# A decoder trunk in float32: the tokens' 1/rms moved from h^T to the projections' results, and the first projection begun K tile by K tile

## The chip, the cores and the metric

One core of one Trainium2 chip runs the whole kernel in one launch. The metric is the device time in microseconds, the median of several runs.

## The reference

Four residual layers on x (256 tokens by 1024 columns, float32). Layers 0 and 3 are of kind A (gated), layer 1 is attention (B), layer 2 pooling (C). What matters here is the norm and kind A:

```python
def rms_norm(x, g):
    y = x * lax.rsqrt(jnp.mean(x * x, axis=-1, keepdims=True) + EPS)
    return y * g

def mixer_a(h, w_in, v_gain, w_s, b_s, w_out):          # h = rms_norm(x, norm_gain[i])
    proj = h @ w_in                                     # 1024 -> 3 * 2048
    u, v, z = ...                                       # 2048 columns each
    v = rms_norm(v, v_gain)
    mixed = jnp.einsum('gij,bcjgd->bcigd', ws, v) + b_s # 8 groups, 128 x 128 lower triangular
    y = u * mixed * jax.nn.silu(z)
    return y @ w_out                                    # x = x + this
```

A token's 1/rms is one number per row of h. It commutes with h @ w_in: a row of the result may be multiplied by it instead.

## The kernel before

**Products.** Every float32 product is made of three matmuls on rounded parts (`mm3`, L75): high by high (L77), high by low (L78), low by high (L79). `hi_of` (L81, ScalarE) makes a high part, `lo_of` (L84, VectorE) the low part from the source and the high one. The stationary operand is a 128x128 tile of h^T (a K tile `k` of 8 and a token block `t` of 2), the moving one 512 columns of weights.

**Weights.** The host lays all weights out as a stream of 272 units of 128x1024 (512 KB): two K tiles of 512 columns each. `load_units` (L127) starts a unit's transfer on SP's queue into one of four raw buffers (`wr`), `split_hi` (L137) makes its high part, `split_units` (L147) its low part and starts the transfer of the unit four further on. `wNh` and `wNl` are the parts of unit N. A projection of 512 columns uses four units, and `step` (L163) keeps the splitting a few units ahead.

**Order.** The program text sets the order of every engine's queue; nothing is reordered on the chip between engines' instructions of one queue. Small generators (`spawn`, `tick`) put the work behind a projection between the products of the next ones.

**The norm.** For each token block: squares of both halves of x on ScalarE (`half_ss`, L205), the sum (L210), the power -1/2 on GpSimd (L212), the scaling of both halves on VectorE (`norm_scale`, L218, tile `xs`), eight transposes on TensorE into PSUM (L227, tile `hp`), then per K tile the high part with the norm's gain on ScalarE (L232) and the low part on VectorE (L235), both into `hT`.

**The start.** SP's queue holds x of token block 0 in two halves, units 0 and 1, x of block 1 in two halves, units 2 and 3. TensorE runs 24 warm-up transposes of the identity (`WARM`). The norm of block 0 is written out with the splitting of units 0 to 4 between its parts (`between`), block 1's norm follows behind `split_hi(3)` and on. The first projection, columns 0 to 511 of v, is skewed (`proj_tok` with `skew`, L259): all eight K tiles of block 0 first, then all eight of block 1; block 1's transposes (`first_t1`) are put in after three ticks, behind the products with unit 2. The loads of v's gain, W_s and b_s (`load_a`, L343) are on GpSimd's queue.

**Layer A.** `v_task` (L367) squares v on ScalarE (L372) and multiplies it by the gain into `vv` (L373), of which high and low parts are made; after the fourth block of columns, GpSimd's power (L392) gives v's 1/rms, which scales W_s into high and low parts `wsr` (L397, L399). `mix_task` multiplies these with v. z goes through Silu (L456). `y_task` multiplies u by silu(z) (L430) and by the mixed v (L433), turns and splits the result for the output projection (`proj_out`, L297).

Of the kernel before, what the change touches and what calls it, by code (L numbers as in the profile page):

```python
# [17 lines left out]
P = 128  # L18
# [23 lines left out]
MIX_LAG = 4  # L42
LAST_LAG = 1
LAST_AHEAD = 3
WARM = 24


@with_exitstack
def hybrid_trunk_kernel(ctx, tc, x, wts, norm_gainT, a_v_gain, a_wsT, a_bsT, b_gl, b_gv, c_scaleT,
# [121 lines left out]

    xt = [cp.tile([P, D], F32, tag=f"x{t}", name=f"x{t}") for t in range(2)]

    def load_x(t):
        for n in range(2):
            nc.sync.dma_start(xt[t][:, n * HALF:(n + 1) * HALF], x[t * P:(t + 1) * P, n * HALF:(n + 1) * HALF])

    load_x(0)
    load_units(2)
    load_x(1)  # L180
    load_units(RAW_BUFS)
    ident = cp.tile([P, P], F32, tag="ident", name="ident")
    make_identity(nc, ident)
    m05_row = cp.tile([P, 32], F32, tag="m05", name="m05")
    nc.gpsimd.memset(m05_row, -0.5)
    m05 = m05_row[:, :4]
    junk = cp.tile([P, HALF + 32], BF16, tag="junk", name="junk")[:, :HALF]
    hT = cp.tile([P, 2 * KT * S + 16], F32R, tag="hT", name="hT")

    def h_parts(layer):  # L190

        o = 16 if layer in (0, DEPTH - 1) else 0
# [22 lines left out]
    def norm_scale(layer, t, r, engs=(nc.vector, nc.vector)):  # L215
        xs = cp.tile([P, 2, HALF], F32, tag="xs", name=f"xs{layer}{t}", bufs=1)
        for n in range(2):
            engs[n].tensor_scalar(xs[:, n], xt[t][:, n * HALF:(n + 1) * HALF], r[:, 0:1], None, op0=ALU.mult)  # L218
        return xs

    def norm_transpose(layer, t, xs):

        pts = []
        for n in range(2):
            pt = (trp if n else atp)(f"hp{layer}{t}{n}").rearrange("p (k c) -> p k c", c=P)
            for k in range(4):
                nc.tensor.transpose(pt[:, k], xs[:, n, k * P:(k + 1) * P], ident)  # L227
            pts.append(pt)
        sl = slice(t * P, (t + 1) * P)
        hTh, hTl = h_parts(layer)  # L230
        for k in range(KT):
            nc.scalar.activation(hTh[:, k, sl], pts[k // 4][:, k % 4], AF.Copy, scale=gT[:, layer, k:k + 1])  # L232
            yield k
        for k in range(KT):
            nc.vector.scalar_tensor_tensor(hTl[:, k, sl], pts[k // 4][:, k % 4], gT[:, layer, k:k + 1],  # L235
                                           hTh[:, k, sl].bitcast(F32), op0=ALU.mult, op1=ALU.subtract)
            yield KT + k

    def norm_task(layer, t, ss):
# [43 lines left out]
    def proj_feat(name):
# [57 lines left out]


    def load_a(layer, j):  # L343
        kc = cp.tile([P, 3 * D], F32, tag="kc", name=f"kc{layer}")
        wsT = kc[:, 2 * D:].rearrange("p (g c) -> p g c", c=P)
        nc.gpsimd.dma_start(kc[:, :2 * D], a_v_gain[j:j + 1, :].partition_broadcast(P))
        nc.gpsimd.dma_start(wsT, a_wsT[j])
        bsT = cp.tile([P, 24], F32, tag="bs", name=f"bs{layer}")[:, :8]
        nc.gpsimd.dma_start(bsT, a_bsT[:, j])

        for g in range(8):
            nc.gpsimd.affine_select(out=wsT[:, g], in_=wsT[:, g], pattern=[[1, P]], compare_op=ALU.is_ge,  # L352
                                    fill=0.0, base=0, channel_multiplier=-1)
        return kc, wsT, bsT

    def layer_a(layer, consts, pl, mid):
        hcur[:] = h_parts(layer)
        kc, wsT, bsT = consts

        def tmp(tag, name, bufs):  # L360
            return pl.tile([P, HALF], F32, tag=tag, name=name, bufs=bufs)
# [5 lines left out]
        def v_task(n, o):  # L367
# [54 lines left out]
        def y_task(n, up, us):  # L422
# [24 lines left out]
            done.add(("y", layer, n))  # L447

        for n in range(4):
            spawn(v_task(n, proj_tok(f"v{layer}{n}", skew=layer if n == 0 else None)))  # L450
# [412 lines left out]
        proj_out(layer, 16, get)  # L863


    sss = [tiny(2, f"ss_{t}") for t in range(2)]
    for n in range(2):
        half_ss(0, n, sss[0])
    r = norm_rms(0, 0, sss[0])
    split_hi(1)  # L870
    xs = norm_scale(0, 0, r)
    split_units(1)
    r1 = []

    def between(i):
        if i == 3:
            split_hi(2)
        if i == 7:
            split_hi(3)
            for n in range(2):  # L880
                half_ss(1, n, sss[1])
            split_hi(4)
        if i == KT + 1:
            split_units(2)
        if i == KT + 5:
            split_units(3)
            r1.append(norm_rms(0, 1, sss[1]))
        if i == KT + 7:
            r1.append(norm_scale(0, 1, r1[0]))
            split_units(4)  # L890

    for i in norm_transpose(0, 0, xs):
        between(i)
    done.add(("h", 0, 0))
    xs = r1[1]

    def first_t1():
        for i in norm_transpose(0, 1, xs):
            pass
        done.add(("h", 0, 1))  # L900
        yield 1

    spawn(first_t1(), 3)
    consts = load_a(0, 0)
    box = {}

    def after_ws():
        spawn(load_b())

    with tc.tile_pool(name="L0", bufs=1, reuse_waits="tile") as pl:  # L910
        layer_a(0, consts, pl, after_ws)
    with tc.tile_pool(name="L1", bufs=1, reuse_waits="tile") as pl:
        layer_b(1, box["b"], pl)
    with tc.tile_pool(name="L2", bufs=1, reuse_waits="tile") as pl:
        consts = load_a(3, 1)
        layer_c(2, pl)
    with tc.tile_pool(name="L3", bufs=1, reuse_waits="tile") as pl:
        layer_a(3, consts, pl, lambda: None)


    last = {}
# [134 lines left out]
```

## Time and profile before

| what | us |
|---|---|
| median of 3 runs | 845.04 (844.78 to 845.10) |
| profiled execution, its own time | 844.66 |
| its span, first to last instruction | 842.9 |
| TensorE busy | 831.3 |
| VectorE busy | 546.5 |
| ScalarE busy | 488.6 |
| GpSimd busy | 57.6 |

The span is what the profile shows; 1.8 us of the execution's time lie outside it. Times in rows are microseconds from the span's start, and "mean ns" is of one instruction. An instruction's duration runs from its start to its result, so that neighbours on one engine overlap; the distance from one start to the next is what it costs in a full queue. The mean granted clock over the span was 0.999 of full speed.

### The profile page before, as it was taken

To read this page: it belongs to the slowest core of one execution; us is meant where nothing else is said; L and a number is where in the kernel's file an instruction comes from. 1 tells how busy PE (TensorE), PEld (TensorE's weight loads), DVE (VectorE), ACT (ScalarE), POOL (GpSimd) and SP (SyncE) were. 2 spreads that over 40 slices of the span, in tenths; PEclk is the share of its full clock that TensorE was granted. 3 is DMA by queue.
4 is the path that set the end of the run, shared out by engine and by line. 5 is a ranking of instruction groups with operands and counts; after the bars stand their busy time and mean duration, and the time that the engine had idled before them with its cause. 6 is when DMAs were issued, how large, how long until landed. Compare 5 with 4: busy or idle time off the path is not lost.

```text
span 842.9 us, 12424 instructions
## 1 busy us (share of the span) xinstructions
PE 831.3 (99%) x4600; PEld 718.2 (85%) x4600; DVE 546.5 (65%) x932; ACT 488.6 (58%) x918; POOL 57.6 (7%) x79
## 2 busy tenths in 40 slices
PE   8999999999999999999999999999999999999998
PEld 6888888888988888888888889999988888888886
DVE  6876556646747667667668576798754776556551
ACT  7665444336758677677678567446543666434340
POOL 1301000001001021021021012000000000000000
PEclk9999999999999999999999999999999999999999
DMA  8766564552754346345345267546664466454541
GB/s 303 271 203 224 190 198 164 187 193 84 254 174 163 112 147 179 121 151 175 126 150 173 78 220 252 181 150 229 218 204 149 138 245 208 158 183 167 175 149 51
DMA packets 41500, 149.57 MB, mean 177 GB/s; under 512 B 4864, under 2 KB 4880, under 8 KB 41184
## 3 DMA queue, kind: packets, MB, share of 16 engines
q1 hardware_dynamic: 40320, 144.72, 51.8%
q0 software_dynamic: 976, 4.05, 1.4%
q8 instruction: 36, 0.59, 0.3%
q14 instruction: 24, 0.20, 0.1%
q10 hardware_dynamic: 144, 0.02, 0.0%
HBM read 147.72 MB, written 1.05 MB: 176 GB/s over the span
## 4 chain that ended last, share of the span: by engine, by line
PE 86%; ACT 7%; DVE 2%; issue 2%; POOL 2%; DMA 0%; POOLq 0%; DVEq 0%; ACTq 0%
PE wo L77 6%; PE wo L79 6%; PE wo L78 6%; PE qk L79 4%; PE qk L77 4%; PE qk L78 4%; PE z L79 3%; PE z L77 3%; PE u L77 3%; PE z L78 3%; PE u L78 3%; PE u L79 3%; PE v L78 3%; PE v L79 3%; PE v L77 3%; ACT junk L508 2%
## 5 line engine op out<-in xcount | busy, mean ns | idle before, releaser
L513 POOL TENSOR_TENSOR qr<-qm,m 128x4 f32<-128x4 f32 x24 | 30.3, 1272 | 224.2 <-DVE qm L512 224.2
L517 ACT ACTIVATE qn<-qk,qr 128x128 f32<-128x128 f32 x96 | 27.5, 382 | 15.1 <-POOL qr L513 15.1
L508 ACT ACTIVATE junk<-qk 128x128 bf16<-128x128 f32 x96 | 26.8, 279 | 7.3 <-PE qk L79 4.6
L430 DVE TENSOR_TENSOR sz<-u,sz 128x512 f32<-128x512 f32 x16 | 11.0, 685 | 28.2 <-PE u L79 28.2
L232 ACT ACTIVATE hT<-hp,gT 128x128 fp32r<-128x128 f32 x64 | 17.5, 383 | 16.1 <-PE hp L227 16.1
L212 POOL TENSOR_TENSOR r<-ms,m 128x1 f32<-128x1 f32 x8 | 5.4, 670 | 284.8 <-DVE ms L210 284.8
L327 DVE TENSOR_TENSOR x<-wo,x 128x512 f32<-128x512 f32 x16 | 11.0, 690 | 20.1 <-PE wo L79 20.0
L235 DVE SCALAR_TENSOR_TENSOR hT<-hp,gT,hT 128x128 fp32r<-128x128 f32 x64 | 17.9, 343 | 7.7 <-ACT hT L232 7.7
L372 ACT ACTIVATE junk<-v 128x512 bf16<-128x512 f32 x16 | 9.6, 600 | 17.8 <-PE v L79 17.6
L508 ACT ACTIVATION_READ_ACCUMULATOR junk<-qk 128x1 f32 x96 | 19.1, 199 | 0.0
L373 DVE TENSOR_TENSOR vv<-v,kc 128x512 f32<-128x512 f32 x16 | 10.8, 688 | 12.4 <-ACT junk L372 12.2
L526 DVE TENSOR_TENSOR ra<-qn,kcb 128x64 f32<-128x64 f32 x48 | 10.6, 221 | 12.0 <-ACT qn L517 10.9
L456 ACT ACTIVATE sz<-z 128x512 f32<-128x512 f32 x16 | 9.5, 598 | 15.3 <-PE z L79 14.7
L538 PE MATMUL qt<-ident,qn 128*128 128x128 f32 x96 | 14.6, 274 | 3.4 <-DVE qk12l L546 0.5
L538 PEld LDWEIGHTS qt<-ident,qn 128*128 128x128 f32 x96 | 11.3, 140 | 7.3 <-issue 2.7
L205 ACT ACTIVATE junk<-x 128x512 bf16<-128x512 f32 x16 | 10.2, 639 | 11.0 <-DVE x L327 9.4
L433 DVE SCALAR_TENSOR_TENSOR yy<-mx,bs,sz 128x256 f32<-128x256 f32 x32 | 14.0, 480 | 0.6
L608 ACT ACTIVATE p<-p,rl 128x384 f32<-128x384 f32 (+1 forms) x16 | 11.5, 769 | 4.8 <-DVE rl L607 4.8
L530 DVE TENSOR_TENSOR rb<-qn,kcb 128x32 f32<-128x32 f32 x96 | 13.7, 183 | 0.0
L604 ACT ACTIVATE p<-p,nb 128x768 f32<-128x768 f32 x8 | 7.5, 938 | 7.9 <-DVE nb L603 7.9
L512 DVE TENSOR_SCALAR qm<-qs 128x4 f32<-128x4 f32 x24 | 3.3, 164 | 12.8 <-ACT junk L508 12.8
L352 POOL TENSOR_SCALAR_AFFINE_SELECT kc<-kc 128x128 f32<-128x128 f32 x16 | 10.0, 659 | 14.1 <-DMA kc<-in_a_wsT_dram 14.1
(2770 smaller groups left out, 3257.8 us busy)
## 6 DMA issues: line engine op xcount, KB each, us to landing
wr<-in_wts_dram SPq DMA_DIRECT2D x272, 512.0 KB, 4.1
kc<-in_a_v_gain_dram POOLq DMA_DIRECT2D x2, 1024.0 KB, 6.4
x<-in_x_dram SPq DMA_DIRECT2D x4, 256.0 KB, 4.7
kc<-in_a_wsT_dram POOLq DMA_DIRECT2D x2, 512.0 KB, 8.2
out_dram<-x SPq DMA_DIRECT2D x4, 256.0 KB, 2.0
kcb<-in_masks_dram POOLq DMA_DIRECT2D x1, 576.0 KB, 8.0
kcb<-in_b_gl_dram POOLq DMA_DIRECT2D x1, 192.0 KB, 5.9
kcb<-in_rope_dram POOLq DMA_DIRECT2D x1, 64.0 KB, 7.9
```

The source lines that it names most:

```text
L77: nc.tensor.matmul(out_ap, lh[0], rh[0], start=start, stop=False, skip_group_check=True)
L78: nc.tensor.matmul(out_ap, lh[0], rh[1], start=False, stop=False, skip_group_check=True)
L79: nc.tensor.matmul(out_ap, lh[1], rh[0], start=False, stop=stop, skip_group_check=True)
L232: nc.scalar.activation(hTh[:, k, sl], pts[k // 4][:, k % 4], AF.Copy, scale=gT[:, layer, k:k + 1])
L235: nc.vector.scalar_tensor_tensor(hTl[:, k, sl], pts[k // 4][:, k % 4], gT[:, layer, k:k + 1], hTh[:, k, sl].bitcast(F32), op0=ALU.mult, op ...
L433: nc.vector.scalar_tensor_tensor(y[:, sl], mxs[n][t][:, sl], bsT[:, 2 * n + gg:2 * n + gg + 1], us[t][:, sl], op0=ALU.add, op1=ALU.mult)
L508: nc.scalar.activation(junk[:, :HD], ov[t][:, h], AF.Square, accum_out=ssq[t][:, h:h + 1])
L513: nc.gpsimd.tensor_tensor(rq[t], ms, m05, op=ALU.pow)
L517: nc.scalar.activation(qn[t][:, h], ov[t][:, h], AF.Copy, scale=rq[t][:, h:h + 1])
L530: nc.vector.tensor_tensor(rb[:, hs, s0:s0 + 16], qn[t][:, hs, s1:s1 + 16], c, op=ALU.mult)
L538: nc.tensor.transpose(pts[t][:, h], qn[t][:, h], ident)
L608: nc.scalar.activation(f, f, AF.Copy, scale=rl[i][:, 0:1])
```

## The change

In the gated layers (0 and 3) h^T is made of x itself with the norm's gain, without the tokens' 1/rms: `norm_scale` returns x. The 1/rms, kept in two columns beside the constant -0.5 (`r_rows`), goes to the results: as the scale of the squares of v, into the factor of W_s (a product of two 1/rms on GpSimd), as the scale of Silu, and into the product of u and silu(z).

In layer 0 the norm then no longer stands ahead of the first products. `proj_first` writes the first projection out: x's first halves of both token blocks are turned, then K tile by K tile the high and low parts of h^T and of the weights (halves of units 0 and 1) are made and both token blocks' products issued; then the second halves are turned, and units 2 and 3 follow whole. The squares and powers come behind. SP's queue takes x's first halves and the halves of unit 0 in turn, then unit 1, then x's second halves; the first 512 columns of v's gain move to SP's queue behind unit 3, and the other constants of layer 0 are loaded after `proj_first`. The warm-up has 13 transposes instead of 24.

```diff
-WARM = 24
+WARM = 13
...
-    load_x(0)
+    raws.append(wp.tile([P, 2, HALF], F32, tag="wr", name="wr0", bufs=RAW_BUFS))
+    loaded[0] += 1
+    for t in range(2):
+        load_x(t, 0)
+        nc.sync.dma_start(raws[0][:, t], wts[0].rearrange("p (k n) -> p k n", n=HALF)[:, t])
     load_units(2)
-    load_x(1)
+    for t in range(2):
+        load_x(t, 1)
     load_units(RAW_BUFS)
+    kc_first = cp.tile([P, 3 * D], F32, tag="kc", name="kc0")
+    nc.sync.dma_start(kc_first[:, :HALF], a_v_gain[0:1, :HALF].partition_broadcast(P))
...
-        r = tiny(1, f"r{layer}{t}")
+        r = r_rows[t] if gated(layer) else tiny(1, f"r{layer}{t}")
+        r_tok[t] = r
...
+    def norm_scale(layer, t, r):
+        if gated(layer):
+            return xt[t].rearrange("p (n c) -> p n c", c=HALF)
...
+    def proj_first(name):
...
+        for t in range(2):
+            turn(t, 0)
+        for u in range(2):
+            w_pair(u)
+            for kk in range(2):
+                k = 2 * u + kk
+                if u == 0:
+                    high(0, 0) if k == 0 else high(1, 1)
+                    high(0, 1) if k == 0 else None
+                    w_high(0, kk)
+                    high(1, 0) if k == 0 else None
+                else:
+                    high(0, k)
+                    high(1, k)
+                    w_high(1, kk)
+                w_low(u, kk)
+                for t in range(2):
+                    low(t, k)
+                products(k)
+        for t in range(2):
+            turn(t, 1)
+        for u in range(2, 4):
+            for k in (2 * u, 2 * u + 1):
+                high(0, k)
+                high(1, k)
+            split_hi(u + 1)
+            split_units(u + 1)
+            for k in (2 * u, 2 * u + 1):
+                low(0, k)
+                low(1, k)
+                products(k)
+        used[0] += 4
+        split_units(5)
+        for t in range(2):
+            ss = tiny(2, f"ss_{t}")
+            for n in range(2):
+                half_ss(t, n, ss)
+            norm_rms(0, t, ss)
+        split_units(6)
+        for t in range(2):
+            done.add(("h", 0, t))
+        for _ in range(8):
+            tick()
+        return o
...
-                nc.scalar.activation(junk, o[t], AF.Square, accum_out=vs[t][:, n:n + 1])
+                nc.scalar.activation(junk, o[t], AF.Square, scale=r_tok[t][:, 0:1], accum_out=vs[t][:, n:n + 1])
...
-                rs.append(r)
+                rr = tiny(1, f"vrr{layer}{t}")
+                nc.gpsimd.tensor_tensor(rr, r, r_tok[t], op=ALU.mult)
+                rs.append(rr)
...
-                nc.vector.tensor_tensor(us[t], up[t], us[t], op=ALU.mult)
+                nc.vector.scalar_tensor_tensor(us[t], up[t], r_tok[t][:, 0:1], us[t], op0=ALU.mult, op1=ALU.mult)
...
-                nc.scalar.activation(sz, zp[t], AF.Silu)
+                nc.scalar.activation(sz, zp[t], AF.Silu, scale=r_tok[t][:, 0:1])
```

`turn` issues the four transposes of a half, `high` and `low` a K tile's parts of h^T, `w_high` and `w_low` those of half a unit, `products` the two blocks' six matmuls of a K tile.

**TensorE, the start of the program, before.** `warm` is the warm-up, `hp000` and `hp001` the turned first and second half of block 0's scaled x, `v00_0` the first projection's PSUM bank of token block 0.

```order
L199 MATMUL warm_87<-ident_78 128x128 x24
L227 MATMUL hp000_131<-ident_78,xs00_125 128x128 x4
L227 MATMUL hp001_136<-ident_78,xs00_125 128x128 x4
L77 MATMUL v00_0_202<-w0h_122,hT_86 128x512
L78 MATMUL v00_0_202<-w0l_123,hT_86 128x512
L79 MATMUL v00_0_202<-w0h_122,hT_86 128x512
```

The same place now; `hp000` and `hp010` are the first halves of blocks 0 and 1, and the transposes read x.

```order
L213 MATMUL warm_90<-ident_81 128x128 x13
L241 MATMUL hp000_111<-ident_81,x0_64 128x128 x4
L241 MATMUL hp010_116<-ident_81,x1_65 128x128 x4
L77 MATMUL v00_0_109<-w0h_121,hT_89 128x512
L78 MATMUL v00_0_109<-w0l_122,hT_89 128x512
L79 MATMUL v00_0_109<-w0h_121,hT_89 128x512
L77 MATMUL v00_1_110<-w0h_121,hT_89 128x512
```

The transposes of the second halves have left this place (they now stand behind the products with unit 1), and block 1's products alternate with block 0's.

**ScalarE, from unit 1 to unit 5, before.** L205 are the squares of x.

```order
L82 ACTIVATE w1h_145<-wr1_70 128x1024
L232 ACTIVATE hT_86<-hp001_136,gT_112 128x128 x4
L82 ACTIVATE w2h_152<-wr2_74 128x1024
L205 ACTIVATE junk_85,ss_1_115<-x1_65 128x512 x2
L82 ACTIVATE w3h_157<-wr3_76 128x1024
L232 ACTIVATE hT_86<-hp010_222,gT_112 128x128 x4
L232 ACTIVATE hT_86<-hp011_227,gT_112 128x128 x4
L82 ACTIVATE w4h_260<-wr4_129 128x1024
L82 ACTIVATE w5h_272<-wr5_163 128x1024
```

The same place now; `hp001` and `hp011` are the second halves. The two rows of h^T parts come twice ahead of w2h and twice ahead of w3h (once each shown ahead of w2h).

```order
L82 ACTIVATE w1h_149<-wr1_71 128x512
L245 ACTIVATE hT_89<-hp001_177,gT_104 128x128
L245 ACTIVATE hT_89<-hp011_182,gT_104 128x128
...
L82 ACTIVATE w2h_191<-wr2_75 128x1024
...
L82 ACTIVATE w3h_217<-wr3_77 128x1024
L82 ACTIVATE w4h_239<-wr4_139 128x1024
L219 ACTIVATE junk_88,ss_0_245<-x0_64 128x512 x2
L219 ACTIVATE junk_88,ss_1_251<-x1_65 128x512 x2
L82 ACTIVATE w5h_257<-wr5_167 128x1024
```

w2h and w3h now stand behind the parts of h^T that the transposes release, and the squares of both blocks behind w4h.

**VectorE, from unit 4 to unit 7, before.** `vv` is v times its gain, `v00l` its low part.

```order
L85 TENSOR_TENSOR w4l_261<-wr4_129,w4h_260 128x1024
L85 TENSOR_TENSOR w5l_273<-wr5_163,w5h_272 128x1024
L85 TENSOR_TENSOR w6l_285<-wr6_170,w6h_284 128x1024
L373 TENSOR_TENSOR vv000_298<-v00_0_202,kc0_184 128x512
L373 TENSOR_TENSOR vv001_299<-v00_1_203,kc0_184 128x512
L85 TENSOR_TENSOR v00l_297<-vv000_298,v00h_296 128x512
L85 TENSOR_TENSOR v00l_297<-vv001_299,v00h_296 128x512
L85 TENSOR_TENSOR w7l_315<-wr7_182,w7h_314 128x1024
```

The same place now:

```order
L85 TENSOR_TENSOR w4l_240<-wr4_139,w4h_239 128x1024
L224 SCALAR_TENSOR_TENSOR ms00_248<-ss_0_245 128x1
L224 SCALAR_TENSOR_TENSOR ms01_254<-ss_1_251 128x1
L85 TENSOR_TENSOR w5l_258<-wr5_167,w5h_257 128x1024
L476 TENSOR_TENSOR vv000_279<-v00_0_109,kc0_79 128x512
L476 TENSOR_TENSOR vv001_280<-v00_1_110,kc0_79 128x512
L85 TENSOR_TENSOR v00l_278<-vv000_279,v00h_277 128x512
L85 TENSOR_TENSOR v00l_278<-vv001_280,v00h_277 128x512
L85 TENSOR_TENSOR w6l_296<-wr6_195,w6h_295 128x1024
```

The sums of the squares have moved in front of w5l, and w6l has moved behind the evacuation of the first projection (on ScalarE w6h likewise).

## Rows read from the trace of the kernel before

**Rows 1.** Page, part 1: busy us (share of span) x instructions.
```profile
PE 831.3 (99%) x4600; PEld 718.2 (85%) x4600; DVE 546.5 (65%) x932; ACT 488.6 (58%) x918; POOL 57.6 (7%) x79
```

**Rows 2.** View of waits, TensorE: us in total, times, longest.
```profile
PE qt L538 <- DVE qk12l L546: 0.5, 1, 0.5
...
PE v L78 <- DVE w2l L85: 0.5, 1, 0.5
```

**Rows 3.** Chain of waits, first 26 us: start, us, what.
```profile
0.81 3.17 DMA x<-in_x_dram
...
4.00 0.73 ACT junk L205 x2
...
14.95 1.14 DVE w3l L85
```

**Rows 4.** Timeline, TensorE, first 25 us: start, us, instruction [idle before].
```profile
1.43 4.39 PE L199 MATMUL warm<-ident 128*128 128x128 f32 x24 [1.43 <-POOL ident masks.py:199]
6.95 1.09 PE L227 MATMUL hp<-ident,xs 128*128 128x128 f32 x8 [1.13 <-DVE xs L218]
8.07 0.51 PE L77 MATMUL v<-w0h,hT 128*128 128x512 f32 x1
...
16.47 0.40 PE L79 MATMUL v<-w3h,hT 128*128 128x512 f32 x1
...
22.84 0.39 PE L77 MATMUL v<-w4h,hT 128*128 128x512 f32 x1
```

**Rows 5.** Windows of TensorE: stretch, busy (count), PEclk, DMA share, GB/s.
```profile
2.40:3.40 1.00, 1.00 (x6) 1.00 0.97 312
4.70:5.70 1.00, 1.00 (x10) 1.00 1.16 299
...
838.90:840.90 2.00, 0.00 (x0) 1.00 0.23 88
840.90:842.90 2.00, 0.00 (x0) 0.51 0.11 43
```

**Rows 6.** Timeline, ScalarE, first 25 us.
```profile
7.65 1.14 ACT L232 ACTIVATE hT<-hp,gT 128x128 fp32r<-128x128 f32 x4
8.66 1.07 ACT L82 ACTIVATE w1h<-wr 128x1024 fp32r<-128x1024 f32 x1
9.61 1.16 ACT L232 ACTIVATE hT<-hp,gT 128x128 fp32r<-128x128 f32 x4
...
23.68 0.62 ACT L82 ACTIVATE v00h<-vv 128x512 fp32r<-128x512 f32 x1
```

**Rows 7.** VectorE: groups by form (busy, mean ns | idle), then timeline.
```profile
L235 DVE SCALAR_TENSOR_TENSOR hT<-hp,gT,hT 128x128 fp32r<-128x128 f32 x16 | 4.5, 343 | 0.4 <-ACT hT L232 0.4
L85 DVE TENSOR_TENSOR v00l<-vv,v00h 128x512 fp32r<-128x512 f32 x2 | 1.4, 696 | 0.1
...
11.95 1.22 DVE L85 TENSOR_TENSOR w2l<-wr,w2h 128x1024 fp32r<-128x1024 f32 x1
...
26.15 1.23 DVE L85 TENSOR_TENSOR w7l<-wr,w7h 128x1024 fp32r<-128x1024 f32 x1 [0.26 <-ACT w7h L82]
```

**Rows 8.** SP's queue: issue of units 0 and 1, their landing; landing of x1's halves.
```profile
1.71 0.90 SPq L131 DMA_DIRECT2D wr<-in_wts_dram  x2
DMA to landing us min/median/max: 4.9/5.4/5.9
...
DMA to landing us min/median/max: 6.1/6.2/6.3
```

**Rows 9.** Timeline: GpSimd's power and selects, W_s's low part, its first matmul.
```profile
13.47 0.56 POOL L212 TENSOR_TENSOR r<-ms,m 128x1 f32<-128x1 f32 x1 [7.10 <-DVE ms L210]
...
24.29 6.93 POOL L352 TENSOR_SCALAR_AFFINE_SELECT kc<-kc 128x128 f32<-128x128 f32 x8 [8.51 <-DMA kc<-in_a_wsT_dram]
...
64.52 1.28 DVE L399 SCALAR_TENSOR_TENSOR wsr01l<-kc,vr,wsr01h 128x1024 fp32r<-128x1024 f32 x1
...
71.80 0.28 PE L77 MATMUL mx<-v00h,wsr00h 128*128 128x256 f32 x1
```

**Rows 10.** Timeline, TensorE: layer 3's first transposes.
```profile
651.74 1.04 PE L227 MATMUL hp<-ident,xs 128*128 128x128 f32 x8
```

More of the change, by code (lines that the diff above doesn't have):

```diff
@@ L172, in hybrid_trunk_kernel, with load_x @@
     xt = [cp.tile([P, D], F32, tag=f"x{t}", name=f"x{t}") for t in range(2)]
-    def load_x(t):
-        for n in range(2):
-            nc.sync.dma_start(xt[t][:, n * HALF:(n + 1) * HALF], x[t * P:(t + 1) * P, n * HALF:(n + 1) * HALF])
-    load_x(0)
+    def load_x(t, n):
+        nc.sync.dma_start(xt[t][:, n * HALF:(n + 1) * HALF], x[t * P:(t + 1) * P, n * HALF:(n + 1) * HALF])
+    raws.append(wp.tile([P, 2, HALF], F32, tag="wr", name="wr0", bufs=RAW_BUFS))
[3 more added lines that the diff above has]
+        nc.sync.dma_start(raws[0][:, t], wts[0].rearrange("p (k n) -> p k n", n=HALF)[:, t])
     load_units(2)
-    load_x(1)
+    for t in range(2):
+        load_x(t, 1)
     load_units(RAW_BUFS)
+    kc_first = cp.tile([P, 3 * D], F32, tag="kc", name="kc0")
+    nc.sync.dma_start(kc_first[:, :HALF], a_v_gain[0:1, :HALF].partition_broadcast(P))
     ident = cp.tile([P, P], F32, tag="ident", name="ident")
@@ L184, in hybrid_trunk_kernel, with gated @@
     m05_row = cp.tile([P, 32], F32, tag="m05", name="m05")
-    nc.gpsimd.memset(m05_row, -0.5)
     m05 = m05_row[:, :4]
+    nc.gpsimd.memset(m05, -0.5)
+    r_rows = [m05_row[:, 8 * t + 8:8 * t + 9] for t in range(2)]
     junk = cp.tile([P, HALF + 32], BF16, tag="junk", name="junk")[:, :HALF]
     hT = cp.tile([P, 2 * KT * S + 16], F32R, tag="hT", name="hT")
+    def gated(layer):
+        return layer in (0, DEPTH - 1)
+    r_tok = [None, None]
     def h_parts(layer):
-        o = 16 if layer in (0, DEPTH - 1) else 0
+        o = 16 if gated(layer) else 0
         return [hT[:, o + i * KT * S:o + (i + 1) * KT * S].rearrange("p (k s) -> p k s", s=S) for i in range(2)]
@@ L217, in norm_scale, with h_turn @@
         for n in range(2):
-            engs[n].tensor_scalar(xs[:, n], xt[t][:, n * HALF:(n + 1) * HALF], r[:, 0:1], None, op0=ALU.mult)
+            nc.vector.tensor_scalar(xs[:, n], xt[t][:, n * HALF:(n + 1) * HALF], r[:, 0:1], None, op0=ALU.mult)
         return xs
-    def norm_transpose(layer, t, xs):
[L223 to L230, printed above, removed]
+    def h_turn(layer, t, n, xs, bank):
+        pt = bank(f"hp{layer}{t}{n}").rearrange("p (k c) -> p k c", c=P)
+        for k in range(4):
+            nc.tensor.transpose(pt[:, k], xs[:, n, k * P:(k + 1) * P], ident)
+        return pt
@@ new lines, in h_high, with h_low @@
+    def h_high(layer, t, k, pt):
+        nc.scalar.activation(h_parts(layer)[0][:, k, t * P:(t + 1) * P], pt[:, k % 4], AF.Copy,
+                             scale=gT[:, layer, k:k + 1])
+    def h_low(layer, t, k, pt):
+        hTh, hTl = (a[:, k, t * P:(t + 1) * P] for a in h_parts(layer))
+        nc.vector.scalar_tensor_tensor(hTl, pt[:, k % 4], gT[:, layer, k:k + 1], hTh.bitcast(F32), op0=ALU.mult,
+                                       op1=ALU.subtract)
+    def norm_transpose(layer, t, xs):
+        pts = [h_turn(layer, t, n, xs, trp if n else atp) for n in range(2)]
@@ L231, in norm_transpose @@
         for k in range(KT):
-            nc.scalar.activation(hTh[:, k, sl], pts[k // 4][:, k % 4], AF.Copy, scale=gT[:, layer, k:k + 1])
+            h_high(layer, t, k, pts[k // 4])
             yield k
         for k in range(KT):
-            nc.vector.scalar_tensor_tensor(hTl[:, k, sl], pts[k // 4][:, k % 4], gT[:, layer, k:k + 1],
-                                           hTh[:, k, sl].bitcast(F32), op0=ALU.mult, op1=ALU.subtract)
+            h_low(layer, t, k, pts[k // 4])
             yield KT + k
@@ L280, in proj_tok, with turn, high, low @@
                 step(kk)
+        return o
+    def proj_first(name):
+        o = [pp(f"{name}_{t}") for t in range(2)]
+        pts = {}
+        def turn(t, n):
+            pts[t, n] = h_turn(0, t, n, norm_scale(0, t, None), trp if t and n else atp)
+        def high(t, k):
+            h_high(0, t, k, pts[t, k // 4])
+        def low(t, k):
+            h_low(0, t, k, pts[t, k // 4])
+        def w_pair(u):
+            units.append(pair(wp, [P, 2, HALF], "w", f"w{u}", W_BUFS))
+            split[0] += 1
+        def w_high(u, kk):
+            hi_of(units[u][0][:, kk], raws[u][:, kk])
+        def w_low(u, kk):
+            lo_of(units[u][1][:, kk], raws[u][:, kk], units[u][0][:, kk])
+            if kk:
+                lowered[0] += 1
+                load_units(u + 1 + RAW_BUFS)
+        def products(k):
+            w = units[k // 2]
+            for t in range(2):
+                mm3(o[t], h_t(k, t), (w[0][:, k % 2], w[1][:, k % 2]), k == 0, k == KT - 1)
+        for t in range(2):
[37 more added lines that the diff above has]
+        split_units(6)
+        for t in range(2):
+            done.add(("h", 0, t))
+        for _ in range(8):
+            tick()
         return o
@@ L343, in load_a @@
     def load_a(layer, j):
-        kc = cp.tile([P, 3 * D], F32, tag="kc", name=f"kc{layer}")
+        kc = kc_first if layer == 0 else cp.tile([P, 3 * D], F32, tag="kc", name=f"kc{layer}")
         wsT = kc[:, 2 * D:].rearrange("p (g c) -> p g c", c=P)
-        nc.gpsimd.dma_start(kc[:, :2 * D], a_v_gain[j:j + 1, :].partition_broadcast(P))
+        n0 = HALF if layer == 0 else 0
+        nc.gpsimd.dma_start(kc[:, n0:2 * D], a_v_gain[j:j + 1, n0:].partition_broadcast(P))
         nc.gpsimd.dma_start(wsT, a_wsT[j])
@@ L357, in layer_a @@
         hcur[:] = h_parts(layer)
-        kc, wsT, bsT = consts
+        first = proj_first(f"v{layer}0") if layer == 0 else None
+        kc, wsT, bsT = consts()
         def tmp(tag, name, bufs):
@@ L449, in layer_a @@
         for n in range(4):
-            spawn(v_task(n, proj_tok(f"v{layer}{n}", skew=layer if n == 0 else None)))
+            spawn(v_task(n, first if first and n == 0 else
+                         proj_tok(f"v{layer}{n}", skew=layer if n == 0 else None)))
         for n in range(4):
@@ L863, in layer_c @@
         proj_out(layer, 16, get)
[L866 to L904, printed above, removed]
     box = {}
@@ L917, in hybrid_trunk_kernel @@
     with tc.tile_pool(name="L3", bufs=1, reuse_waits="tile") as pl:
-        layer_a(3, consts, pl, lambda: None)
+        layer_a(3, lambda: consts, pl, lambda: None)
     last = {}
```

3 lines of the change are left out of this document (1 added, 2 removed).

## The prediction

> **What bounds the kernel now.** Read part 1 of the page first: TensorE is busy 99% of the span, VectorE and ScalarE some 60% [rows 1]. Time can only be won where TensorE waits, and the view of waits names the places [rows 2]: the start, four waits of the first projection for low halves of weights (one is shown), and in layer B seven of 0.5 us for queries and keys (one shown), which the change does not touch. The chain of waits over the first 26 us tells what sets the start [rows 3]: x lands at 3.98, the squares, the power, the scaling and the transposes follow one another, and the last link that is not TensorE's is the low half of w3, done at 16.1. From there on the chain is matmul after matmul. So I follow one mark: the first product with w4, at 22.84 [rows 4]. Behind it TensorE's work keeps its order and its number of matmuls; if nothing new waits there, the end moves by as much as this mark.
>
> Between the first product at 8.07 and the mark stand 48 products at 0.227 us (28 steps from 16.47 to 22.84 [rows 4]), 10.9 us, and eight transposes, some 0.9 us; the other 3 us of the 14.8 are waits.
>
> **The start.** The first x half is still the first transfer and lands at 3.98 [rows 3]. Thirteen warm-up transposes take TensorE to about 4.25: ten start in a microsecond after 4.7 and about half as many before [rows 5], so 0.21 each from 1.43. That is 0.27 past the landing. Removed from here are two squares, a power and a scaling, 4.00 to 6.9. The four transposes of a half cost 0.70 until ScalarE runs (6.95 to 7.65 [rows 4, 6]), here 0.85, since the clock doubles only at 4.7: ScalarE begins at 5.1. Two high parts of h^T at 0.25 (four from 7.65 to 8.66) and half of w0's high part, 0.62 as for v00h [rows 6], give the first product at 6.25, 1.8 earlier. VectorE then needs 0.70 for the low half of 512 columns and 0.34 for a low part of h^T [rows 7]: the third product starts at 7.3, and 22 more times 0.227 end the 24 products of the first four K tiles at 12.3; I take 12.35.
>
> This holds only if the transfers keep up. w0 landed 4.9 after its issue at 1.71, and w1, issued right behind at 2.2, after 5.9: at 6.6 and 8.1 [rows 8]. The bytes ahead of the second half of w0, and of w1, are the same after the change. ScalarE wants them at 6.7 and, for TensorE not to wait, by 8.3. x1's first half was never third in line: it must land between 3.98 and 6.6; by its bytes, two thirds of the way, I take 5.6 and keep both ends. Per K tile ScalarE needs 1.1 (two high parts, half a w) and VectorE up to 1.4 against TensorE's 1.36, so neither falls behind by much.
>
> **The middle.** The second x halves are turned only after those 24 products, at 12.35. Then stand in series: 0.70 for the transposes, four high parts (the second waits for the other bank, 0.4 later) until 14.2, all of w2h, 1.07 as for w1h, all of w2l, 1.22, and a low part, 0.34 [rows 6, 7]. The product that needs that low part starts at 16.85; TensorE has one product to do meanwhile and is idle for some 3 us. This is the new wait that takes the place of the old ones. 22 products later, at 21.85, comes the mark: **1.0 us earlier**. w3l is done at 18.6, just as the products with w2 end.
>
> **Behind the mark.** The four squares of x, 0.73 each [rows 3], now stand on ScalarE between w4h and w5h, and w6 has moved behind the evacuation of v00. ScalarE is busy without a gap from w2h on: a w takes 0.95 to its successor (8.66 to 9.61 [rows 6]), so w2h, four high parts, w3h, w4h and the squares bring w5h to 21.0 and w5l's end to 23.3, needed at 24.8. The first product with the gain, 0.70, lets v00h start at 24.0. From v00h to the low half of the next w took 2.47 before (23.68 to 26.15 [rows 6, 7]), and that half takes 1.22: w6l is done at 27.4 to 27.7, needed at 27.5. I count nothing, but there is no margin: what ScalarE loses here TensorE loses too. w7 has over 1 us to spare.
>
> **What costs nothing.** GpSimd's loads of the rest of v's gain, of W_s and b_s now stand behind both powers; the second of these moves from 13.47 to about 21.3, and so do the selects, from 24.29 to 32 and their end from 31.2 to 39, 24 us ahead of wsr [rows 9]. The gain, ahead of W_s in that queue, is there by 32 too, and v's second block reads it after its products end at 32.7. SP's extra load (256 KB) stands before w4, which ScalarE wants only at 17. The product of the two 1/rms adds two steps of some 0.6 on GpSimd ahead of wsr; its last part ended at 65.8 and its second matmul group waits until 71.8 [rows 9]; with that cover of 6 us gone it would cost 1.2. The 16 gate products take the form with a scalar: W_s's low part in that form takes 1.28 for 1024 columns, w2l in the other 1.22 [rows 7, 9], so 0.03 more for 512, beside TensorE. Layer 3 loses its scalings, but its transposes at 651.74 already start without a wait [rows 10]: nothing gained.
>
> **Sum.** The profiled execution took 844.66, 0.38 below the median of the runs, 845.04. Less 1.0 that is 843.7, and on the scale of the median **844.0**. A measurement of this kernel tells about 0.2%, 1.7 us, from no change; 1.0 is within it.
>
> **Rivals.**
>
> The clock falls in the middle wait, and the kernel **ends slower than before**. At the program's end the granted clock reads 1.00 for two microseconds without a matmul and then 0.51, that is 1.2 GHz [rows 5]. The gap of 1.13 us ahead of the transposes at 6.95 did not lower it: eight of them still took 1.09 [rows 4]. The new wait is 2.0 idle, one product, 0.9 idle, between the two. If the clock falls, a product takes twice 0.227 until it is back. At the start it was back some 3.2 us after the work began (1.43 to 4.7): 3.2 us hold 7 products instead of 14, 1.6 lost, and 844.0 becomes 845.6. [...] The Trainium skill (TensorE: Matmul & The Clock Gate, section "HAM oscillation — how this bites in real kernels") says that waits between bursts of products throw the array back to half clock and that each new burst starts slow. By that rule 845.6 is the result; the trace agrees with it at the program's end and not in the gap before 6.95. Chance 0.28, with 0.04 of it for two such stretches, 847.2.
>
> The halves land late. If x1's first half comes only at 6.6, its high parts, the second half of w0h and of w0l follow a microsecond later, and the first 24 products end at 13.2: 844.9, no gain. For it: x1's halves took 6.1 from their issue [rows 8]. Against: 1.5 MB were ahead of them then, and only 512 KB now. Chance 0.12.
>
> The middle wait is short. The durations contain latencies that neighbours overlap (1.07 for a w on ScalarE, 0.95 to the next; 1.14 for four high parts, 1.01 to the next); if the two fills run at spacings, both shrink by some 0.4, and the gain is 1.8: 843.2. Were the middle wait gone altogether, 3 us more, 841.0. Against: each link there waits for the one before. Chance 0.15.
>
> **How the numbers follow.** Forecast 0.45, 844.0, with 843.2 to 844.9 of its own. Faster by over 0.2% (below 843.35): the short wait, 0.15, and 0.03 from the forecast's edge, 0.18. Slower by over 0.2% (above 846.7): two stretches at the low clock, 0.04, and 0.02 for late landings together with one, 0.06. The rest, 0.76, is within 0.2%. The range 842.4 to 846.0 takes in the forecast, late landings, one stretch at the low clock and the nearer half of the short wait.
>
> **What would show it.** First product near 6.25; TensorE without gaps from 7.3 to 12.4; then some 3 us of wait for the low half of w2; the first product with w4 near 21.9; no wait for w6; the clock at 1.00 to the end. A mark near 23.4, with products 0.45 apart behind the middle wait, is the clock; high parts of token block 1 that wait for x are the landings; a middle wait under 2.2 us is the third rival. A new wait of TensorE after 30 us, or a mark later than 24, would make the whole account wrong.

## The result, and the profile of the changed kernel

The changed kernel takes **848.61 us** (median of 5 runs, 848.51 to 849.38), the kernel before on the same chip 845.1 (5 runs, 844.78 to 845.76): a ratio of 1.0043 [1.0028, 1.0057]. It is 0.43% slower, where 844.0 in a range of 842.4 to 846.0 was forecast. The profiled execution took 848.61 with a span of 846.9, 4.0 more than before.

Part 1 of the page, against [rows 1]: TensorE is still busy nearly throughout, with 11 transposes fewer.

```profile
PE 833.9 (98%) x4589; PEld 718.5 (85%) x4589; DVE 544.2 (64%) x926; ACT 492.2 (58%) x920; POOL 53.1 (6%) x83
```

The view of waits of TensorE, against [rows 2] (waits in total, times, longest). The waits of layer B have stayed; at the start there are a wait for the high part of w2, which ScalarE makes, one for its low part, two each for w0l and w1l, and one for w6l.

```profile
PE v L77 <- ACT w2h L82: 1.9, 1, 1.9
...
PE v L78 <- DVE w2l L85: 0.8, 1, 0.8
PE v L78 <- DVE w1l L85: 0.5, 2, 0.2
PE v L78 <- DVE w0l L85: 0.4, 2, 0.2
...
PE v L78 <- DVE w6l L85: 0.2, 1, 0.2
```

TensorE's timeline, against [rows 4]. The first product is at 6.55; then each K tile begins 2.17 us behind the last (6.55, 8.72, 10.89, 13.05, the last not shown), though its six products need 1.36. The first 24 products end at 15.08, the mark, the first product with w4, is at 26.27.

```profile
4.26 1.06 PE L241 MATMUL hp<-ident,x 128*128 128x128 f32 x4
5.56 1.11 PE L241 MATMUL hp<-ident,x 128*128 128x128 f32 x4 [0.24 <-DMA x<-in_x_dram]
6.55 0.50 PE L77 MATMUL v<-w0h,hT 128*128 128x512 f32 x1
...
8.72 0.50 PE L77 MATMUL v<-w0h,hT 128*128 128x512 f32 x1
9.45 0.49 PE L78 MATMUL v<-w0l,hT 128*128 128x512 f32 x1 [0.22 <-DVE w0l L85]
...
10.89 0.50 PE L77 MATMUL v<-w1h,hT 128*128 128x512 f32 x1
...
15.08 1.03 PE L241 MATMUL hp<-ident,x 128*128 128x128 f32 x8
18.03 0.49 PE L77 MATMUL v<-w2h,hT 128*128 128x512 f32 x1 [1.92 <-ACT w2h L82]
19.29 0.50 PE L78 MATMUL v<-w2l,hT 128*128 128x512 f32 x1 [0.77 <-DVE w2l L85]
19.63 0.42 PE L79 MATMUL v<-w2h,hT 128*128 128x512 f32 x1
...
23.76 0.40 PE L78 MATMUL v<-w3l,hT 128*128 128x512 f32 x1
...
26.27 0.39 PE L77 MATMUL v<-w4h,hT 128*128 128x512 f32 x1
...
31.71 0.39 PE L77 MATMUL v<-w6h,hT 128*128 128x512 f32 x1
32.30 0.50 PE L78 MATMUL v<-w6l,hT 128*128 128x512 f32 x1 [0.20 <-DVE w6l L85]
```

The reason stands in the other two engines' timelines. ScalarE, against [rows 6]:

```profile
4.05 1.28 ACT L245 ACT_TABLE_LOAD   x1 [4.05 <-DMA gT<-in_norm_gainT_dram]
5.36 0.62 ACT L245 ACTIVATE hT<-hp,gT 128x128 fp32r<-128x128 f32 x2
...
8.05 0.62 ACT L82 ACTIVATE w0h<-wr 128x512 fp32r<-128x512 f32 x1
9.69 0.63 ACT L245 ACTIVATE hT<-hp,gT 128x128 fp32r<-128x128 f32 x2 [1.02 <-DVE hT L250]
10.21 0.62 ACT L82 ACTIVATE w1h<-wr 128x512 fp32r<-128x512 f32 x1
...
16.92 1.06 ACT L82 ACTIVATE w2h<-wr 128x1024 fp32r<-128x1024 f32 x1
20.05 1.14 ACT L245 ACTIVATE hT<-hp,gT 128x128 fp32r<-128x128 f32 x4 [2.07 <-DVE hT L250]
21.08 1.06 ACT L82 ACTIVATE w3h<-wr 128x1024 fp32r<-128x1024 f32 x1
```

VectorE, against [rows 7]:

```profile
8.70 0.69 DVE L85 TENSOR_TENSOR w0l<-wr,w0h 128x512 fp32r<-128x512 f32 x1 [0.95 <-ACT w0h L82]
9.31 0.60 DVE L250 SCALAR_TENSOR_TENSOR hT<-hp,gT,hT 128x128 fp32r<-128x128 f32 x2
10.87 0.69 DVE L85 TENSOR_TENSOR w1l<-wr,w1h 128x512 fp32r<-128x512 f32 x1 [0.95 <-ACT w1h L82]
...
18.01 1.23 DVE L85 TENSOR_TENSOR w2l<-wr,w2h 128x1024 fp32r<-128x1024 f32 x1 [3.77 <-ACT w2h L82]
19.16 1.12 DVE L250 SCALAR_TENSOR_TENSOR hT<-hp,gT,hT 128x128 fp32r<-128x128 f32 x4
22.17 1.23 DVE L85 TENSOR_TENSOR w3l<-wr,w3h 128x1024 fp32r<-128x1024 f32 x1 [1.90 <-ACT w3h L82]
...
31.02 1.23 DVE L85 TENSOR_TENSOR w6l<-wr,w6h 128x1024 fp32r<-128x1024 f32 x1 [0.26 <-ACT w6h L82]
```

Read the two together as one circle. ScalarE makes half of w0h (8.05), VectorE its low part (8.70) and the low parts of h^T (from 9.31); only when the first of these is done does ScalarE begin the high parts of the **next** K tile (9.69), after a wait of 1.02 for `DVE hT`; behind them comes its half of w1h (10.21), and VectorE has meanwhile waited 0.95 for that. Two engines that could work side by side take turns: 8.70 to 10.87 is 2.17. The high parts need nothing that VectorE's low parts write. What they share is where they read: the four K tiles of a token block's half lie in one PSUM bank (tile `hp`), and here ScalarE reads it for tile k+1 after VectorE has read it for tile k. The same happens to the second halves: the high parts of K tiles 6 and 7 wait 2.07, and w3h and w3l come late.

The clock fell as well. Windows of the changed kernel (stretch, busy in us and count of TensorE, of weight loads, VectorE, ScalarE and GpSimd, then PEclk, DMA share, GB/s): 0.51 of full speed, 1.2 GHz, from 20.2 to 23.4. Before that TensorE was idle for 1.92 us, ran one product, was idle for another 0.77 and had taken up the products again at full clock.

```profile
20.20:23.40 3.20, 3.20 (x9) 2.43 (x8) 1.30 (x3) 3.20 (x7) 0.00 (x0) 0.51 0.50 164
24.00:26.00 2.00, 2.00 (x10) 1.68 (x9) 1.64 (x5) 1.94 (x7) 0.21 (x1) 1.00 0.79 258
```

So there were three theories. **A**: the bank is handed from ScalarE to VectorE and back for every K tile, and that is the loss. **B**: the low clock is. **C**: something else holds the K tiles apart: transfers, or the tile `hT` that both engines write.

### The profile page after: what moved, and what is told of

It reads as the page before. It is cut to its first block, busy times and chain, and to the rows that moved or that the text cites. A ratio compares the mean times of both kernels' runs of the same rounds, so it can differ in the third digit from the quotient of the medians.

```text
span 846.9 us, 12399 instructions
## 1 busy us (share of the span) xinstructions
PE 833.9 (98%) x4589; PEld 718.5 (85%) x4589; DVE 544.2 (64%) x926; ACT 492.2 (58%) x920; POOL 53.1 (6%) x83
## 4 chain that ended last, share of the span: by engine, by line
PE 85%; ACT 8%; DVE 2%; issue 2%; POOL 2%; POOLq 0%; DVEq 0%; ACTq 0%
PE wo L77 6%; PE wo L79 6%; PE wo L78 6%; PE qk L79 4%; PE qk L77 4%; PE qk L78 4%; PE z L79 3%; PE z L77 3%; PE u L77 3%; PE z L78 3%; PE u L78 3%; PE u L79 3%; PE v L78 3%; PE v L79 3%; PE v L77 3%
## 5 line engine op out<-in xcount | busy, mean ns | idle before, releaser
L535 DVE SCALAR_TENSOR_TENSOR sz<-u,m,sz 128x512 f32<-128x512 f32 x16 | 11.9, 746 | 26.8 <-PE u L79 26.8
L562 ACT ACTIVATE sz<-z,m 128x512 f32<-128x512 f32 x16 | 10.7, 687 | 13.8 <-PE z L79 13.8
L475 ACT ACTIVATE junk<-v,m 128x512 bf16<-128x512 f32 x16 | 11.0, 685 | 12.0 <-PE v L79 11.7
L227 POOL TENSOR_TENSOR r<-ms,m 128x1 f32<-128x1 f32 x4 | 3.1, 785 | 173.3 <-DVE ms L224 173.3
L227 POOL TENSOR_TENSOR m<-ms,m 128x1 f32<-128x1 f32 x4 | 2.2, 554 | 123.3 <-DVE ms L224 123.3
```

Source lines behind the costliest of these rows:

```text
L535: nc.vector.scalar_tensor_tensor(us[t], up[t], r_tok[t][:, 0:1], us[t], op0=ALU.mult, op1=ALU.mult)
```

## The experiments

Times are medians beside the kernel before on the same chip (845.1 to 845.4 there); "the end of the 24" is where the first four K tiles' products end, "the mark" the first product with w4 in the profile.

| kernel | end of the 24 | mark | low clock behind the middle wait | us | ratio to before |
|---|---|---|---|---|---|
| before | – | 22.84 | – | 845.1 | 1 |
| forecast | 12.35 | 21.85 | – | 844.0 | – |
| the change | 15.08 | 26.27 | 3.4 | 848.61 | 1.0043 [1.0028, 1.0057] |
| e1: banks of the first halves | 12.68 | 25.05 | 6.8 | 847.35 | 1.0024 [1.0015, 1.0033] |
| e2: TensorE kept busy | 15.28 | 26.32 | 0 | 848.76 | 1.0039 [1.0026, 1.0053] |
| e3: 1/rms moved, old start | – | 22.87 | – | 844.81 | 0.9993 [0.9984, 1.0002] |
| e4: early table load | 15.20 | 26.41 | 3.4 | 848.8 | 1.0039 [1.0026, 1.0052] |
| e6: banks of all halves | 12.60 | 23.34 | 3.4 | 845.11 | 1.0001 [0.9992, 1.001] |
| e7: e6, kept busy | 12.54 | 21.90 | 0 | 844.19 | 0.999 [0.9982, 0.9999] |
| e5: banks and a new order | 14.65 | 20.29 | 0 | 840.89 | 0.9952 [0.994, 0.9965] |
| e9: e5 again | 13.75 | 19.33 | 0 | 841.66 | 0.9955 [0.994, 0.997] |
| e8: the new order, one bank | 14.96 | 20.77 | 0 | 842.8 | 0.997 [0.9958, 0.9981] |

(In e5, e8 and e9 the end contains 0.8 us for the second halves' transposes, which stand ahead of the fourth K tile's products there.) The mark tells the time: profiled time less mark is 821.7 to 821.9 in before, e1, e3, e5, e6, e7, e8 and e9, and 822.3 to 822.4 in the change, e2 and e4, which alone wait for w6l.

**e1: odd K tiles of the first halves in banks of their own.** The second halves' transposes and everything else stay as they are.

```diff
-            pts[t, n] = h_turn(0, t, n, norm_scale(0, t, None), trp if t and n else atp)
+            for k in range(4):
+                if k < 2:
+                    bank = trp if t and k else atp
+                    pts[t, k] = bank(f"hp0{t}{n}{k}").rearrange("p (k c) -> p k c", c=P)
+                else:
+                    pts[t, k] = pts[t, k - 2]
+                nc.tensor.transpose(pts[t, k][:, k], xs[:, n, k * P:(k + 1) * P], ident)
```

> Theory A (PSUM bank): ScalarE's high part of the next K tile waits until VectorE's low part of the last K tile has finished reading the same PSUM bank; with odd K tiles of the first halves in banks of their own, a K tile takes some 1.4 us instead of 2.17, the first 24 products end near 12.7 instead of 15.1, the first product with w4 comes near 23.9 instead of 26.3, and the time falls by some 2.3 us to about 846.3. Theory B (the clock lost in the middle wait is the cause): K tiles still take 2.17 us and the time stays near 848.6. Theory C (the K tiles are paced by the transfers of the half units, or by the shared tile hT that both engines write): no change either, 848.6.

The 24 products end at 12.68, 2.40 earlier, with the same transfers and the same tile `hT`: A holds, and C falls for both of its causes. But the mark came only 1.2 earlier, at 25.05, where 23.9 was expected, and the time of 847.35 is 1.0 above the 846.3 expected. TensorE's timeline shows why: the products behind the middle wait stand 0.43 apart, the clock being at 0.50 to 0.51 in the windows from 16 to 22: twice as long as in the change.

```profile
12.68 1.03 PE L241 MATMUL hp<-ident,x 128*128 128x128 f32 x8
...
16.89 0.79 PE L78 MATMUL v<-w2l,hT 128*128 128x512 f32 x1 [0.77 <-DVE w2l L85]
17.49 0.63 PE L79 MATMUL v<-w2h,hT 128*128 128x512 f32 x1
17.91 0.63 PE L77 MATMUL v<-w2h,hT 128*128 128x512 f32 x1
...
25.05 0.39 PE L77 MATMUL v<-w4h,hT 128*128 128x512 f32 x1
```

**e2: the change with TensorE kept busy.** 26 transposes of the identity into an unused bank behind the second halves' transposes.

```diff
             turn(t, 1)
+        fill = atp("fill")
+        for _ in range(26):
+            nc.tensor.transpose(fill[:, :P], ident, ident)
```

> 26 transposes of the identity fill the middle wait, so that the clock has no reason to fall. Theory B: the eight products that took 0.43 take 0.227, the time falls by 1.6 us to about 847.0. Theory A: the products with w3 wait for the low half of w3, which ScalarE's and VectorE's order sets and the clock does not; the first product with w4 comes at most 0.3 us earlier, the time is 848.3 to 848.6.

The clock stays at 1.00, and nothing is won: 848.76, mark 26.32. The products with w2 are through by 22.2, but then TensorE waits for w3l, whose source is late by the bank:

```profile
16.15 3.00 PE L362 MATMUL fill<-ident 128*128 128x128 f32 x26
...
22.40 0.49 PE L77 MATMUL v<-w3h,hT 128*128 128x512 f32 x1
23.66 0.50 PE L78 MATMUL v<-w3l,hT 128*128 128x512 f32 x1 [0.76 <-DVE w3l L85]
...
26.32 0.39 PE L77 MATMUL v<-w4h,hT 128*128 128x512 f32 x1
```

In the change 23.76 was the start of that product, with the low clock. B falls as the cause of this loss: the low clock filled a wait that was there anyway.

**e3: the 1/rms moved to the results, the start as before.** The cut shown is against the kernel before.

```diff
     def norm_scale(layer, t, r):
+        if gated(layer):
+            return xt[t].rearrange("p (n c) -> p n c", c=HALF)
...
-                nc.scalar.activation(junk, o[t], AF.Square, accum_out=vs[t][:, n:n + 1])
+                nc.scalar.activation(junk, o[t], AF.Square, scale=r_tok[t][:, 0:1], accum_out=vs[t][:, n:n + 1])
```

and likewise in Silu, the product of u and silu(z), and the factor of W_s.

> The 1/rms moved to the results in both gated layers, but layer 0 begun as in the kernel before (whole units, block after block, 24 warm-up transposes). If the move itself costs (scaled forms on ScalarE and VectorE, the product on GpSimd): above 847. Theories A and B both put the loss into the K tile order of the start: 844.5 to 845.3, the first product with w4 near 22.8.

844.81, mark 22.87: this half of the change alone costs nothing and, without the new start, brings nothing that can be told from the noise. The first transposes start earlier (5.89), but the first product waits 1.83 for a part of h^T, which stands behind the whole of w0h on ScalarE, and w0h waited for its transfer:

```profile
7.39 1.06 ACT L82 ACTIVATE w0h<-wr 128x1024 fp32r<-128x1024 f32 x1 [2.20 <-DMA wr<-in_wts_dram]
```

**e4: ScalarE's table loaded early.** In the change the table load stands behind the transfer of the gain and ends at 5.33.

```diff
+    nc.scalar.activation(junk[:, :4], m05, AF.Copy)
```

> A copy of four columns ahead of everything on ScalarE, so that its table is loaded near 1.5 and not at 4.05 behind the wait for the gains. Theory A: the chain of the start begins with ScalarE's first high part, so the first product comes 0.26 us earlier, at 6.3, and the K tiles keep their distance of 2.17: 848.3. If the start hangs on x1's landing or on w0 instead, the first third of a microsecond is lost again: 848.6.

A miss. ScalarE's timeline shows the load at 1.25, and the first high part at 5.36, as in the change: it waits for the transposes, which take 1.06. The first product, at 6.73, stands behind block 1's transposes, and these waited 0.64 for x; so the start hangs on x1's landing here, the other case of the expectation.

```profile
1.25 1.28 ACT L216 ACT_TABLE_LOAD   x1 [1.25 <-PEq L1111]
...
5.36 0.63 ACT L246 ACTIVATE hT<-hp,gT 128x128 fp32r<-128x128 f32 x2 [2.60 <-PE hp L242]
```

and TensorE's:

```profile
5.96 1.11 PE L242 MATMUL hp<-ident,x 128*128 128x128 f32 x4 [0.64 <-DMA x<-in_x_dram]
```

**e6 and e7: own banks for the second halves too, and the same with TensorE kept busy.** K tiles 4 and 5 of a block lie in one bank, 6 and 7 in another; the order is the change's. e7 adds 14 transposes of the identity, 1.7 us, in the middle wait.

```diff
+            banks = [(trp if t and j else atp)(f"hp0{t}{n}{j}").rearrange("p (k c) -> p k c", c=P) for j in range(2)]
             for k in range(4):
+                pts[t, 4 * n + k] = banks[k // 2 if n else k % 2]
...
             turn(t, 1)
+        for _ in range(14):
+            nc.tensor.transpose(pts[1, 6][:, 0], ident, ident)
```

> As e1_banks, and the second halves' K tiles 4, 5 and 6, 7 in different banks too; order and middle wait as in the change. Theory A: the high parts of K tiles 6 and 7 no longer wait for low parts, w3l is done near 19.1 instead of 21.0, and the products with w3 no longer hide what the clock takes. With the clock at full speed the first product with w4 comes near 22.3 and the time is 844.6; with one stretch at the low clock behind the middle wait 24 and 846.2, with two as in e1_banks's profile 25 and 847.3; so a wide spread of the runs, slower where the clock is lower. Theory C (transfers or hT): as e1_banks, 847.3.

> As e6_banks2, with 14 transposes of the identity in the middle wait. If the clock falls because of that wait, and costs once the banks no longer hide it, the runs come together at 844.6, the first product with w4 near 22.4, clock 1.00. If the clock costs nothing here either, the time is that of e6_banks2.

In e6 the high parts of K tiles 6 and 7 start at 15.16 without a wait (ScalarE's timeline), w3l is no longer late, and the time is the kernel's before:

```profile
15.16 1.15 ACT L245 ACTIVATE hT<-hp,gT 128x128 fp32r<-128x128 f32 x4
```

Now the clock does cost: with the filling the mark moves from 23.34 to 21.90 and the median from 845.11 to 844.19. The 0.92 of the medians is small beside e6's spread of 3.1. That spread goes with the clock: six of e6's eleven executions have a mean granted clock of 1.0 and take 844.6 in the mean (843.68 to 845.21), the other five 0.996 to 0.997 and 846.0 (845.02 to 846.74). e6's profile is one of the latter, which may be why the two profiles differ by more, 1.44. TensorE's timeline of e7:

```profile
16.87 0.42 PE L79 MATMUL v<-w2h,hT 128*128 128x512 f32 x1
...
21.90 0.39 PE L77 MATMUL v<-w4h,hT 128*128 128x512 f32 x1
```

That is the forecast's account: 16.85, 21.85 and 844.0 were its numbers.

**e5, e9 and e8: a new order.** The second halves are turned ahead of the fourth K tile's products, w2h stands ahead of their high parts and all of these ahead of w3h; w6 moves ahead of the evacuation, the table is loaded early, and even and odd K tiles have own banks. e9 is the same kernel again; e8 has no `odd`, so that a first half lies in one bank.

```diff
+        even = [pp(f"hp0{t}e") for t in range(2)]
+        odd = [atp(f"hp0{t}o") for t in range(2)]
+        late = [atp("hp00l"), trp("hp01l")]
...
+                if k == 3:
+                    for t in range(2):
+                        turn(t, 1)
                 products(k)
+        split_hi(3)
         for t in range(2):
-            turn(t, 1)
...
+            for k in range(4, 8):
+                high(t, k)
+        split_units(3)
```

> Each token block's even K tiles, odd K tiles and second half in a bank of their own; the second halves turned ahead of the products of the fourth K tile; w2h ahead of the high parts of the second halves, all of these ahead of w3h; the squares behind w5h and w6 ahead of the evacuation of v00; ScalarE's table loaded early. Theory A (banks) with the order of the middle: no wait over 0.3 us between the first products and those with w4, which begin near 19, 3.8 before the kernel before: 841.3 to 842. If the start is paced by ScalarE's and VectorE's work as such (their sum for 8 K tiles and 4 units, some 11 us from 5.4), w4 comes near 20: 842.5. Theory B (the clock is what costs): without a middle wait it has no reason to fall, same time as A; with falls of the clock 843 or more.

> The new order of e5_order, but with all four K tiles of a first half in one PSUM bank again, as in the change; this asks what of the 4.3 us is the order and what the banks. Theory A (the bank is handed from ScalarE to VectorE and back for every K tile): K tiles stand 2.17 us apart again, the first 24 products end near 15.0 with the second halves' transposes among them (in e5_order near 13.2 to 14.6), but the wait for w2 stays short, since highs, w2h and w2l of the second halves do not stand behind those products; the first product with w4 is near 21.0 to 21.6 and the time near 842.0 (841.5 to 842.6), so the banks are worth some 1.1 us here and the order the rest. Rival: the order hides the hand-over altogether, and the time is within 0.4 of e5_order. Rival two: without own banks the order gives nothing, and the time is above 846.

> The kernel of e5_order once more, on the same chip as e8_one_bank, so that the two can be compared: 840.9 (840.6 to 841.6), ratio near 0.995; the first product with w4 at 19.8 to 20.3. In the profile of e5_order the second half of w0 landed late and TensorE waited 0.49 us for it; if that was an accident of one execution, the wait is absent or short here.

e5 is the best version, 4.3 us faster than before (e9, the same kernel, 3.7, a little short of its expectation). Its median, 840.89, lies a little below the 841.3 to 842 that theory A gave, but its mark, 20.29, lies later than the 19 expected; the profiled execution was its slowest, 842.04. Beside layer B's waits TensorE waits in that execution 0.5 for half of w0, which landed late (ScalarE waits 1.38 for it), 0.5 for its low parts, and 0.4 for x. In e9's profile that half was in time, and x's first half of block 1 came later, so late landings move from run to run. e8 shows the K tiles 2.16 apart once more (8.54 to 10.70), and takes 842.8 (842.43 to 843.39) against e9's 841.66 (840.80 to 842.25, four runs) on the same chip: the banks are worth 1.1 in this order, as theory A expected, though the time is 0.2 above its range and the mark, 20.77, 0.2 before its own. The end of the 24 comes 1.2 earlier with own banks (14.96 and e9's 13.75), where e1 had 2.40. Without own banks the order still gives 2.6 against before. The mark of e9 is at 19.33. TensorE's timeline of e8:

```profile
8.54 0.51 PE L77 MATMUL v<-w0h,hT 128*128 128x512 f32 x1
...
10.70 0.50 PE L77 MATMUL v<-w1h,hT 128*128 128x512 f32 x1
...
20.77 0.39 PE L77 MATMUL v<-w4h,hT 128*128 128x512 f32 x1
```

## Why the prediction was wrong

The sign was wrong, and the sum failed at one step: "Per K tile ScalarE needs 1.1 (two high parts, half a w) and VectorE up to 1.4 against TensorE's 1.36, so neither falls behind by much." Both loads are near what the rows show, but they were taken to run side by side. In the bank they share they run in turn, and a K tile costs 2.17; with own banks the 24 products take 6.13 (e1, 6.55 to 12.68), where the sum had 6.10.

- **The start.** First product forecast 6.25, found 6.55. The warm-up ended as counted (4.26), but the four transposes took 1.06, where 0.85 was counted: they start every 0.21 to the end, and block 1's at 5.56 were no faster (1.11 for four). The sum had the clock double at 4.7; the granted clock reads 1.00 on both sides of that time [rows 5], and what the rows show to change there in the kernel before is how often transposes start. The table load, which the sum had left out, ends at 5.33, as late as the transposes (5.32); taking it away alone changed nothing (e4).
- **The first four K tiles.** Forecast end 12.35, found 15.08: 0.30 of it the start, 2.43 the hand-over. With own banks 12.68 (e1).
- **The middle wait** was right: 4.5 from the end of the 24 to the third product with w2, found 19.63 less 15.08, 4.55.
- **From there to the mark** 5.0 was forecast, 6.64 found: w3l, forecast 18.6, ended at 23.40, again by the bank: ScalarE's wait of 2.07 for the low parts of K tiles 4 and 5 stands ahead of w3h.
- **w6** was given no margin and no price: w6l ended 5.98 behind the mark, needed 5.67; TensorE's distance to before grew from 3.43 to 3.92 there.

Together 0.30, 2.43, 0.05 and 1.64 turn the mark's −1.0 into +3.4, and w6 adds 0.5: 3.9, the difference of the profiled executions (848.61 less 844.66 is 3.95). "A new wait of TensorE after 30 us, or a mark later than 24, would make the whole account wrong" was the line that told it, and both came (the wait for w6l at 32.30, the mark at 26.27); no rival named this cause.

Of the rivals, the low clock did come, at the place and with the spacing foreseen. The time that hung on it, 845.6, has no bearing on the change, where it cost nothing (e2). Where the banks are out of the way it costs 0.9 by the medians (e6, e7). The rule of the Trainium skill quoted there agrees with the trace on the fall, but not on the slow start of a burst: in the change the products behind the wait began at full clock, and the granted clock read 1.00 until 20.2. The halves were not late in the change: block 1's transposes waited 0.24 for x, and started at 5.56, where 5.6 was forecast for its landing. The middle wait was not short. What was said to cost nothing, the moved 1/rms, costs nothing (e3).

The trace of before had the sign, two rows that the prediction did not use. VectorE's and ScalarE's timelines of before, at the evacuation of the first projection:

```profile
23.82 0.69 DVE L373 TENSOR_TENSOR vv<-v,kc 128x512 f32<-128x512 f32 x1 [1.18 <-ACT junk L372]
```

```profile
23.59 0.20 ACT L372 ACTIVATION_READ_ACCUMULATOR junk<-v 128x1 f32 x1
```

`vv` does not read what the squares write; both read the same bank of v, and VectorE waits 1.18 until ScalarE has ended at 23.79 (the first 0.36 of it are for v's last product, which ends at 23.00). The four high parts of a bank then stood in one row of four [rows 6] ahead of the low parts, so the bank changed hands once, and no high part of h^T waited for a low one. The change makes it change hands at every K tile. The Trainium skill (PSUM — Partial Sum Buffer, section "PSUM bank collisions raise a hardware error") says that two engines must not access the same bank and the same group of 32 partitions at one time, two readers included, and that semaphores should guard the bank, not the address. The waits on `DVE hT` here agree, 1.02 and 2.07; a collision itself was not tried. Every bank is also one tile of the program here, so the runs show that the shared tile costs the time, and not whether the chip or the program's bookkeeping by tiles asks for the turn-taking.

Left open is the share of each part of the new order in e8's gain: reordered transposes, w2, w6 and the table load were not run one by one in that order.

## What to carry to other kernels

When two engines read one PSUM bank and an edit interleaves them more finely, count the bank as a third party: a group costs about the sum of both engines' steps (2.17 here), not the longer one, unless neighbouring groups lie in different banks. Look for that in the trace before the edit, in any wait of one reader for another that writes nothing it needs. And judge a low clock by what comes due next: in these runs it cost time only where TensorE's products, not another engine's parts, ended last.

## What the runs showed of the chip that was not expected

- A low clock that is free: 3.4 us at 1.2 GHz in the change, with no difference in time from e2's 1.00 throughout.
- The mean granted clock of one program differs from execution to execution: 1.0 in six of e6's eleven runs, 0.996 to 0.997 in the others.
- Products can start at half their rate while the granted clock reads 1.00: in e4 those from 7.87 to 9.58 stand 0.43 apart. It cost little there: the mark is 26.41, and 26.27 in the change.
- The gate product of u in the form with a scalar takes 746 ns for 128x512, the plain form before took 685: 0.06 more, where 0.03 was counted. It lies beside TensorE. The row is of the page, part 5:

```profile
L535 DVE SCALAR_TENSOR_TENSOR sz<-u,m,sz 128x512 f32<-128x512 f32 x16 | 11.9, 746 | 26.8 <-PE u L79 26.8
```
